# First layer's modulation on quarters of TensorE's columns, with a fixed order of the first products

## The chip, the cores and the metric

The kernel runs on one core of a Trainium2 chip. The metric is the device time of one execution in microseconds (us). Below, PE is TensorE, DVE VectorE, ACT ScalarE, POOL GpSimd, and SP the engine whose queue issues nearly all DMAs.

## The reference, cut to what matters

The reference is a network of two blocks of two layers each, on 256 context tokens and 256 latent tokens with 1024 channels, in float32. Only the very beginning matters here. Two conditioning vectors (one for the latents, one for the context) are turned into six modulation vectors of 1024 values by a product with a 1024 x 6144 matrix; the first two of these, shift and scale, go into the first norm, whose result is the input of the first projection:

```python
c_act = jax.nn.silu(c)
cc_act = jax.nn.silu(c_ctx)
for l in range(DEPTH):
    mod = (c_act @ w_mod[l] + b_mod[l])[:, None, :]
    modc = cc_act @ w_mod[l] + b_mod[l]
    sh1, sc1, g1, sh2, sc2, g2 = jnp.split(mod, 6, axis=-1)
    shc1, scc1, gc1, shc2, scc2, gc2 = jnp.split(modc, 6, axis=-1)
    px = (rmsnorm(x, norm1_g[l]) * (1.0 + sc1) + sh1) @ w_in[l] + b_in[l]
    pc = (rmsnorm(xc, norm1_g[l]) * (1.0 + scc1) + shc1) @ w_in[l] + b_in[l]
    ...
```

The gates of a linear recurrence (mLSTM), its keys, queries and values, a gated unit over groups and a convolution are columns of that projection.

## The kernel before, in words

Channels lie on partitions, tokens on the free axis: the input is eight tiles `xT` of 128 x 512 (columns 0 to 255 context, 256 to 511 latents). A projection splits its weights and its input into a high and a low part (`whi`, `wlo`, `aH`, `aL`; L391 loads a tile of weights, L392 and L397 split it) and does three products for each pair of pieces (`mm3`, L411 to L413). The program is written with a framework that orders each engine's instructions by a priority (the place in the program's text, moved by `high_priority(offset=...)`) and by when it believes them to be ready; the result is one fixed order for each engine, with semaphore waits. `issue_after(ins)` adds nothing but an order: what its block puts on the engine of `ins` is queued behind `ins`.

The stage in question is `start` (from L198), followed by `mixer1(0, ...)`:

- `__init__` loads small constants (L105 to L113, all on SP's queue); `start` loads two rows with the conditioning vectors (`crow`, L207) and the eight tiles `xT` (L210). `cvec_pe` (L138, L139) spreads the conditioning vectors over all partitions by products with a row of ones, and ACT applies the silu; the result `cv` is what the dot products on DVE need.
- The statistics of the first norm: squares on ACT (L212), their sum on DVE (L217), a sum over partitions on PE (`npc`, L323), a chain of small DVE operations (`rsq`, from L294), a product that spreads the factor by token (`npb`, L331), and eight products `xr` on DVE (L242).
- The modulation comes in pairs of tiles of 128 values, numbered q = 0 to 3, for scale (part 1) and shift (part 0). All scales and the pair 1 of the shifts are done by `mod_pe`: two weight blocks `mn` of 512 KB (L177), four products each (L180) with two columns stationary and 256 values streamed, so eight accumulating products into a 2 x 256 row `pR`, a copy by ACT (`mrow`, L182), two transposes on PE (`pM`, L184), and `mod_take` on DVE (L191, L196). The other six tiles of shifts are done by `mod_tile`: a block of 512 KB (L162) and one long DVE dot product for each of the two streams (L165).
- For each q ACT then applies scale and shift (`xn`, L255), and `split_plain` gives `aH` and `aL` (L378, L379). Eight buffers `mn` serve all these weight blocks. The first three weight tiles of the projection (`self.pre`) are loaded after pair 1.
- In `mixer1` the first three outputs (the gates, k0 and k1, called p3 below) are accumulated together by `accA`: eight input tiles x three outputs x three products, 72 products of 512 columns. Then `evac` takes the gates, a chain of small operations on DVE and ACT forms running sums and maxima (L727 to L765), and PE spreads them (`ptr`, L764, `pmi`, L759). The projection's further outputs follow in the order of `PLAN[0]`.
- The parts 2, 3 and 5 of the first layer's modulation (24 tiles, two dot products each on DVE, L165, blocks `mw`) are queued in `self.bg` and emitted by `work`. Part 4 is done by `mods`, with the same `mod_pe`, at a priority lowered by `LOW` = 300.

Of the kernel before, what the change touches and what calls it, by code (L numbers as in the profile page):

```python
# [18 lines left out]
D = 1024  # L19
KT = 8  # L20
# [10 lines left out]
# columns of the per-partition vectors of a layer of the first block  # L31
# [14 lines left out]
# constants  # L46
CS = {"ident": (0, 128), "mf": (128, 128), "mb": (256, 128)}
NCS = 384
# [14 lines left out]
SHPE = (1,)  # L63
# [24 lines left out]
class Net:  # L88
    def __init__(self, ctx, tc, i, o):
# [12 lines left out]
        self.late, self.long, self.pre, self.begun = [], None, [], []  # L102
        self.bg, self.credit, self.fence = [], 0.0, None
# [7 lines left out]
        nc.sync.dma_start(out=self.gn, in_=i["gn"])  # L111
        self.mb_t = g.tile([128, 4, 48], F32, name="modb")
        nc.sync.dma_start(out=self.mb_t, in_=i["modb"])  # L113
# [11 lines left out]
    # ---- modulation vectors: n on partitions, one dot product along the free axis each  # L125
# [5 lines left out]

    def cvec_pe(self, s, row):
        """The same for the first block, spread by the tensor engine."""
        nc = self.nc
        t = self.cv[s] = self.mp.tile([128, D], F32, tag="cv", name=f"cv0{s}")
        for h in range(2):
            p = self.mm_tile("pcv")
            nc.tensor.matmul(out=p, lhsT=self.ones[0:1, :], rhs=row[0:1, 512 * h:512 * h + 512], start=True, stop=True)  # L138
            nc.scalar.activation(out=t[:, 512 * h:512 * h + 512], in_=p, func=AF.Silu)  # L139
# [32 lines left out]
    def mod_pe(self, c, q, room, pr, pm):  # L172
        """Tiles 2 q and 2 q + 1 of the first layer's part c on the tensor engine, for both streams: rows, then turned."""
        nc = self.nc
        for h in range(2):
            w = room()
            nc.sync.dma_start(out=w, in_=self.i["modn"][PE_C.index(c), q, h])  # L177
            for n in range(4):
                k = 4 * h + n
                nc.tensor.matmul(out=pr, lhsT=self.cols[:, 2 * k:2 * k + 2], rhs=w[:, 256 * n:256 * n + 256], start=k == 0, stop=k == KT - 1)  # L180
        row = self.np_.tile([128, 256], F32, tag="xn", name="mrow")[0:2, :]
        nc.scalar.copy(out=row, in_=pr)  # L182
        for j in (0, 1):
            nc.tensor.transpose(out=pm[:, 2 * (2 * q + j):2 * (2 * q + j) + 2], in_=row[:, 128 * j:128 * j + 128], identity=self.ident[0:2, 0:2])  # L184
# [1450 lines left out]
```

## Time and profile before

| what | before |
|---|---|
| median of 3 runs (lowest, highest) | 2061.7 us (2060.18, 2063.29) |
| span of the profiled execution | 2055.1 us |
| median of the runs less that span | 6.6 us |
| PE busy, share of the span | 98% |
| DVE, ACT, POOL busy, share of the span | 75%, 45%, 4% |

The span reaches from the first to the last instruction of one profiled execution, and the page gives no other time for it; what a run's time has beyond it lies outside the instructions. A busy time is the union of an engine's instructions. PE's instructions overlap in it, since a product's record begins before the one ahead of it has ended: how fast PE works is read from the distance between starts, or from the length of a row of many.

### The profile page before, as it was taken

The numbers are of one execution on the slowest core, as the hardware profiler recorded it, in microseconds if no ns is written. First come the engines' busy times: TensorE is split into PE (matmuls) and PEld (weight loads), VectorE is DVE, ScalarE is ACT, GpSimd is POOL, SyncE is SP. The second block draws the span as 40 slices with busy tenths as digits, with TensorE's granted clock in tenths as the row PEclk, the third lists the DMA queues.
The fourth block names the chain that finished last, engine by engine and source line by source line (L and its number), as shares of the span: only waits on it lengthen the run. The fifth ranks groups of instructions, "written<-read, shape, count | busy, mean of one in ns | idle before, by whom it ended". The sixth has DMA issues, their size and how long they took to land.

```text
span 2055.1 us, 34137 instructions
## 1 busy us (share of the span) xinstructions
PE 2010.6 (98%) x13196; PEld 1784.5 (87%) x13196; DVE 1545.2 (75%) x3105; ACT 924.5 (45%) x1612; POOL 85.7 (4%) x103
## 2 busy tenths in 40 slices
PE   8999999999999899999999999999999999999999
PEld 3798779888888799999998789888888889999999
DVE  6997789987898768987877667777653487788554
ACT  4324544222322346744556675322222266666443
POOL 0000010000001000200100002000000200001000
PEclk9999999999999999999999999999999999999999
DMA  7532265678766332576651015446752231216554
GB/s 295 181 103 92 97 232 176 211 248 295 235 216 198 111 102 94 170 263 212 202 171 61 22 41 186 154 149 223 260 170 71 70 112 64 73 54 224 182 157 134
DMA packets 98182, 324.22 MB, mean 158 GB/s; under 512 B 11418, under 2 KB 14234, under 8 KB 98020
## 3 DMA queue, kind: packets, MB, share of 16 engines
q1 hardware_dynamic: 98020, 322.04, 47.7%
q8 instruction: 104, 1.70, 0.3%
q14 instruction: 58, 0.48, 0.1%
HBM read 320.95 MB, written 1.05 MB: 157 GB/s over the span
## 4 chain that ended last, share of the span: by engine, by line
PE 89%; DVE 6%; ACT 2%; DMA 1%; issue 1%; SPq 0%; POOL 0%; ACTq 0%; POOLq 0%; DVEq 0%
PE pg L411 6%; PE pd L411 6%; PE pd L413 6%; PE pd L412 6%; PE pu L413 6%; PE pg L412 6%; PE pu L412 6%; PE pg L413 6%; PE pu L411 6%; PE pin L411 5%; PE pin L413 5%; PE pin L412 5%; PE pov L1223 2%; PE ptq L1127 2%; DVE wlo L397 1%; PE po L411 1%
## 5 line engine op out<-in xcount | busy, mean ns | idle before, releaser
L392 ACT CAST whi<-wraw 128x1024 fp32r<-128x1024 f32 (+2 forms) x443 | 429.5, 973 | 797.0 <-PE pu L412 188.9
L397 DVE TENSOR_TENSOR wlo<-wraw,whi 128x1024 fp32r<-128x1024 f32 (+2 forms) x443 | 502.5, 1138 | 155.0 <-ACT whi L392 152.3
L165 DVE CUSTOM_DVE_ANT_0 junk<-mw,cv,modb 128x1024 bf16<-128x1024 f32 x272 | 349.6, 1285 | 51.3 <-DMA mw<-in_modw 45.2
L411 PE MATMUL pd<-hH,whi 128*128 128x256 f32 (+1 forms) x748 | 245.4, 328 | 0.0
L412 PE MATMUL pd<-hL,whi 128*128 128x256 f32 (+1 forms) x748 | 245.1, 328 | 0.0
L413 PE MATMUL pd<-hH,wlo 128*128 128x256 f32 (+1 forms) x748 | 244.8, 327 | 0.0
L411 PE MATMUL pg<-aH,whi 128*128 128x256 f32 (+1 forms) x704 | 233.8, 332 | 0.3 <-ACT aH L374 0.3
L413 PE MATMUL pu<-aH,wlo 128*128 128x256 f32 (+1 forms) x704 | 233.5, 332 | 0.3 <-DVE wlo L397 0.3
L412 PE MATMUL pg<-aL,whi 128*128 128x256 f32 (+1 forms) x704 | 233.6, 332 | 0.0
L412 PE MATMUL pu<-aL,whi 128*128 128x256 f32 (+1 forms) x704 | 233.2, 331 | 0.0
L411 PE MATMUL pu<-aH,whi 128*128 128x256 f32 (+1 forms) x704 | 233.2, 331 | 0.0
L413 PE MATMUL pg<-aH,wlo 128*128 128x256 f32 (+1 forms) x704 | 233.2, 331 | 0.0
L412 PEld LDWEIGHTS pd<-hL,whi 128*128 128x128 f32 x748 | 142.2, 190 | 12.2
L411 PEld LDWEIGHTS pd<-hH,whi 128*128 128x128 f32 x748 | 142.4, 190 | 12.0
L413 PEld LDWEIGHTS pd<-hH,wlo 128*128 128x128 f32 x748 | 142.2, 190 | 12.0
L411 PE MATMUL pin<-whi,aH 128*128 128x256 f32 x512 | 150.0, 293 | 1.4 <-ACT aH L374 1.1
L412 PE MATMUL pin<-wlo,aH 128*128 128x256 f32 x512 | 148.0, 289 | 0.0
L413 PE MATMUL pin<-whi,aL 128*128 128x256 f32 x512 | 147.2, 289 | 0.3 <-DVE aL L375 0.2
L411 PEld LDWEIGHTS pg<-aH,whi 128*128 128x128 f32 x704 | 133.7, 190 | 13.2 <-ACT aH L374 0.5
L413 PEld LDWEIGHTS pu<-aH,wlo 128*128 128x128 f32 x704 | 133.7, 190 | 13.1 <-DVE wlo L397 0.5
L413 PEld LDWEIGHTS pg<-aH,wlo 128*128 128x128 f32 x704 | 133.8, 190 | 12.6
L412 PEld LDWEIGHTS pg<-aL,whi 128*128 128x128 f32 x704 | 133.8, 190 | 12.5
(339 smaller groups left out, 4150.8 us busy)
## 6 DMA issues: line engine op xcount, KB each, us to landing
wraw<-in_wgu SPq DMA_DIRECT2D x176, 512.0 KB, 4.4
mw<-in_modw SPq DMA_DIRECT2D x168, 512.0 KB, 4.2
wraw<-in_win SPq DMA_DIRECT2D x92, 512.0 KB, 3.5
wraw<-in_wdn SPq DMA_DIRECT2D x64, 384.0 KB, 3.5
wraw<-in_wout SPq DMA_DIRECT2D x47, 512.0 KB, 3.5
wraw<-in_wdn SPq DMA_DIRECT2D x64, 320.0 KB, 3.4
mn<-in_modn SPq DMA_DIRECT2D x18, 512.0 KB, 5.6
mn<-in_modw SPq DMA_DIRECT2D x6, 512.0 KB, 7.3
```

The costliest lines, as they stand in the source:

```text
L165: r = nc.vector.tensor_tensor_reduce(out=junk, in0=w, in1=self.cv[s], scale=1.0, scalar=self.mb_t[:, 2 * b + l, j:j + 1], op0=ALU.mult, op ...
L392: nc.scalar.copy(out=hi[:, :n], in_=raw[:, :n])
L397: nc.vector.tensor_tensor(out=lo[:, :n], in0=raw[:, :n], in1=hi[:, :n], op=ALU.subtract)
L411: mm(out=out, lhsT=wh, rhs=xh, start=start, stop=False)
L412: mm(out=out, lhsT=wh, rhs=xl, start=False, stop=False)
L413: mm(out=out, lhsT=wl, rhs=xh, start=False, stop=stop)
L1127: nc.tensor.transpose(out=pt[:, h, :], in_=a.bitcast(F32).rearrange("p e d -> p (e d)"), identity=self.ident)
L1223: nc.tensor.matmul(out=po[64 * b:64 * b + 64, e // 2, :], lhsT=vN[:, kc, 64 * g:64 * g + 64], rhs=u["PT"][:, kc, :], start=kc == 0, stop=k ...
```

## The change

`mod_pe` no longer accumulates its eight products into one row of two partitions. It writes four products at a time to the four quarters (32 partitions each) of the output, with stationary operands padded with zeros to 32 columns (`columns`), and accumulates only over the two weight blocks; two products with a constant of two columns (`quart`), which has ones at the partitions 32 n + s, then add the four partial sums and turn the row at once, in place of the transposes. In `start` all eight tiles of the shifts are done in this way too, so `start` has no dot products on DVE, and the conditioning vectors spread over the partitions are not made there: two broadcast loads and two silus (`cvecs(0)`) make them, at the head of `self.bg`, with a priority lowered by 150. Each pair's products are queued on PE behind those of the pair before; 18 of p3's products (those of the input tiles 0 and 1) are queued between the pairs 2 and 3, and the other 54 behind pair 3. ACT's work for pair 2 is queued behind the last split of the three weight tiles. The constants' loads move from SP's queue to ACT's. The diff's core (comments, which it also removes, are left out):

```diff
-        self.cols = g.tile([128, 4 * KT], F32, name="cols")
+        self.cols = g.tile([128, KT, 2], F32, name="cols")
         nc.sync.dma_start(out=self.cols, in_=i["ccol"])
-        nc.scalar.activation(out=self.cols, in_=self.cols, func=AF.Silu)
...
-        nc.sync.dma_start(out=self.cst, in_=i["cst"])
+        nc.scalar.dma_start(out=self.cst, in_=i["cst"])
...
+    def columns(self, pool):
+        t = pool.tile([128, KT, 32], F32, name="cols32")
+        self.nc.gpsimd.memset(t, 0.0)
+        self.nc.vector.tensor_copy(out=t[:, :, 0:2], in_=self.cols)
+        return t
...
-    def mod_pe(self, c, q, room, pr, pm):
+    def mod_pe(self, cols, c, q, room, pr, pm):
         nc = self.nc
         for h in range(2):
             w = room()
             nc.sync.dma_start(out=w, in_=self.i["modn"][PE_C.index(c), q, h])
             for n in range(4):
-                k = 4 * h + n
-                nc.tensor.matmul(out=pr, lhsT=self.cols[:, 2 * k:2 * k + 2], rhs=w[:, 256 * n:256 * n + 256], start=k == 0, stop=k == KT - 1)
-        row = self.np_.tile([128, 256], F32, tag="xn", name="mrow")[0:2, :]
+                nc.tensor.matmul(out=pr[32 * n:32 * n + 32, :], lhsT=cols[:, 4 * h + n, :], rhs=w[:, 256 * n:256 * n + 256],
+                                 start=h == 0, stop=h == 1)
+        row = self.np_.tile([128, 256], F32, tag="xn", name="mrow")
         nc.scalar.copy(out=row, in_=pr)
         for j in (0, 1):
-            nc.tensor.transpose(out=pm[:, 2 * (2 * q + j):2 * (2 * q + j) + 2], in_=row[:, 128 * j:128 * j + 128], identity=self.ident[0:2, 0:2])
+            r = nc.tensor.matmul(out=pm[:, 2 * (2 * q + j):2 * (2 * q + j) + 2], lhsT=row[:, 128 * j:128 * j + 128], rhs=self.C("quart"),
+                                 start=True, stop=True)
+        return r.ins
...
-            for s, row in enumerate(rows):
-                self.cvec_pe(s, row)
...
-            def scale(q):
-                for c in (1, 0) if q in SHPE else (1,):
+            cols = self.columns(mf)
+            def part(q):
+                for c in (1, 0):
...
-            def shift(j):
-                if j // 2 not in SHPE:
-                    self.mod_tile(0, 0, j, (1, 0), room())
-            for j in range(2):
-                shift(j)
-            scale(0)
+            last = part(0)
             npb = self.rstd_rows([acc], T, 1.0 / D, pc, pb)
...
             for q in range(4):
-                with self.tc.issue_after(npb.ins):
-                    if q:
-                        scale(q)
-                for j in (2 * q, 2 * q + 1):
-                    if j >= 2:
-                        shift(j)
+                if q == 3:
+                    p3 = [self.mm_tile("pin") for _ in self.pre]
+                    with self.tc.issue_after(last):
+                        last = self.accA(p3, self.pre, (self.aH[:2], self.aL[:2]), ALL, True, False)
+                if q:
+                    with self.tc.issue_after(last):
+                        last = part(q)
                 if q == 1:
                     self.pre = [self.weights(self.i["win1"][0][j]) for j in range(3)]
-                for k in (2 * q, 2 * q + 1):
+                with ExitStack() as after:
+                    if q == 2:
+                        after.enter_context(self.tc.issue_after(self.whi))
+                    for k in (2 * q, 2 * q + 1):
...
+            self.first = (p3, last)
...
-                    p3 = [self.mm_tile("pin")[:, :cs[1] - cs[0]] for _ in w3]
-                    self.accA(p3, w3, (self.aH, self.aL), cs)
+                    if last:
+                        p3 = [self.mm_tile("pin")[:, :cs[1] - cs[0]] for _ in w3]
+                        self.accA(p3, w3, (self.aH, self.aL), cs)
+                    else:
+                        p3, ins = self.first
+                        with tc.issue_after(ins):
+                            self.accA(p3, [[a[:, 256:] for a in w] for w in w3], (self.aH[2:], self.aL[2:]), cs, False)
...
             def mods():
                 pm = self.mm_tile("pm")
+                cols32 = self.columns(tp)
                 for q in range(4):
-                    self.mod_pe(4, q, lambda: self.mp.tile([128, D], F32, tag="mw", bufs=2, name="mn"), pm[0:2, 0:256], pm[:, 256:272])
+                    self.mod_pe(cols32, 4, q, lambda: self.mp.tile([128, D], F32, tag="mw", bufs=2, name="mn"), pm[:, 0:256], pm[:, 256:272])
...
         self.start()
+        def vectors():
+            with self.tc.high_priority(offset=-150):
+                self.cvecs(0)
+        self.bg.append((0, vectors, None))
         self.mod_queue(0, 0, [j for j in range(16, 48) if j // 8 not in PE_C], (0, 1))
```

## Rows read from the trace of the kernel before

**Rows 1.** The profile's page: busy us by engine, share of the span, instructions.

```profile
PE 2010.6 (98%) x13196; PEld 1784.5 (87%) x13196; DVE 1545.2 (75%) x3105; ACT 924.5 (45%) x1612; POOL 85.7 (4%) x103
```

**Rows 2.** Stages (from:to, length): busy PE, PEld, DVE, ACT, POOL, clock, DMA, GB/s.

```profile
0.00:20.00 20.00, 12.14 (x24) 5.25 (x25) 10.17 (x17) 7.99 (x14) 0.91 (x7) 1.00 0.85 300
120.00:160.00 40.00, 40.00 (x268) 36.98 (x268) 40.00 (x89) 9.12 (x10) 0.00 (x0) 1.00 0.27 90
270.00:300.00 30.00, 26.05 (x199) 25.32 (x198) 28.27 (x48) 13.22 (x18) 5.54 (x6) 0.94 0.79 263
```

**Rows 3.** PE in order of time (start, length, instructions), 0 to 58 us.

```profile
4.35 7.16 PE L138 MATMUL pcv<-crow,ones 1*128 1x512 f32 x8 [4.35 <-DMA crow<-in_cvec]
14.77 1.86 PE L323 MATMUL npc<-ones,sqa 128*128 128x1 f32 x8 [3.25 <-DVE sqa L217]
16.89 5.87 PE L180 MATMUL pR<-mn,cols 128*2 128x256 f32 x16 [0.26 <-DMA mn<-in_modn]
24.48 3.62 PE L180 MATMUL pR<-mn,cols 128*2 128x256 f32 x16
46.18 0.50 PE L411 MATMUL pin<-aH,whi 128*128 128x512 f32 x1
...
57.63 0.39 PE L413 MATMUL pin<-aH,wlo 128*128 128x512 f32 x1
```

**Rows 4.** The same, the first part's weight loads (PEld), 17 to 18 us.

```profile
17.27 0.13 PEld L180 LDWEIGHTS pR<-mn,cols 128*2 128x2 f32 x1 [0.30 <-issue]
17.70 0.13 PEld L180 LDWEIGHTS pR<-mn,cols 128*2 128x2 f32 x1 [0.30 <-issue]
```

**Rows 5.** DMA, 0 to 75 us: rate in 40 slices of 1.875 us; issues by line.

```profile
GB/s 5 155 194 309 300 326 398 419 415 404 415 411 406 409 417 406 402 417 354 288 385 415 380 42 0 0 0 0 35 218 305 398 48 267 256 339 258 13 229 50
mn<-in_modn SPq DMA_DIRECT2D x10, 512.0 KB, 8.8
mn<-in_modw SPq DMA_DIRECT2D x6, 512.0 KB, 7.3
```

**Rows 6.** SP's queue in order of time: the first issue, and those of xT.

```profile
0.75 0.39 SPq L105 DMA_DIRECT2D cols<-in_ccol  x1
3.26 3.67 SPq L210 DMA_DIRECT2D xT<-in_xT  x8
```

**Rows 7.** PE late in the first mixer: products with 64 columns, then with 128.

```profile
218.24 1.09 PE L924 MATMUL psg<-sws,vs 128*64 128x128 f32 x16
219.26 1.09 PE L862 MATMUL pht<-cst,hs 128*128 128x128 f32 x8
```

**Rows 8.** In order of time, ACT and PE: three weight splits; a part's copy and turn.

```profile
28.73 2.93 ACT L392 CAST whi<-wraw 128x1024 fp32r<-128x1024 f32 x3
45.18 0.36 ACT L182 COPY mrow<-pR 2x256 f32<-2x256 f32 x1 [0.73 <-PE pR L180]
45.97 0.28 PE L184 MATMUL pM<-cst,mrow 2*128 2x2 f32 x2
```

**Rows 9.** Stages, dot products of L165 alone: DVE busy us (two records each).

```profile
0.00:52.50 52.50, 15.47 (x24) 1.00 0.77 288
52.50:58.00 5.50, 3.88 (x6) 1.00 0.55 184
```

**Rows 10.** The gates' chain in order of time: dot products in it, PE's wait.

```profile
65.62 1.27 DVE L165 CUSTOM_DVE_ANT_0 junk<-mw,cv,modb 128x1024 bf16<-128x1024 f32 x1
75.58 1.28 DVE L165 CUSTOM_DVE_ANT_0 junk<-mw,cv,modb 128x1024 bf16<-128x1024 f32 x1
77.68 0.28 PE L764 MATMUL ptr<-cst,RT 100*128 100x100 f32 x1 [3.31 <-issue]
```

**Rows 11.** Part 4 in the mixer, PE in order of time: a run, then single products.

```profile
222.33 2.75 PE L180 MATMUL pm<-mn,cols 128*2 128x256 f32 x12
251.98 0.59 PE L180 MATMUL pm<-mn,cols 128*2 128x256 f32 x2
252.82 0.59 PE L180 MATMUL pm<-mn,cols 128*2 128x256 f32 x2
```

More of the change, by code (lines that the diff above doesn't have):

```diff
@@ L45 @@
 NR2 = 776
-CS = {"ident": (0, 128), "mf": (128, 128), "mb": (256, 128)}
-NCS = 384
+CS = {"ident": (0, 128), "mf": (128, 128), "mb": (256, 128), "quart": (384, 2)}
+NCS = 386
 CG = {"sel": (0, 512), "reset": (512, 512)}
@@ L62 @@
 PE_C = [0, 1, 4]
-SHPE = (1,)
 WPRI = {"m1": 50, "ev": 400}
@@ L102, in __init__ @@
         self.late, self.long, self.pre, self.begun = [], None, [], []
+        self.whi = None
         self.bg, self.credit, self.fence = [], 0.0, None
-        self.cols = g.tile([128, 4 * KT], F32, name="cols")
+        self.cols = g.tile([128, KT, 2], F32, name="cols")
         nc.sync.dma_start(out=self.cols, in_=i["ccol"])
-        nc.scalar.activation(out=self.cols, in_=self.cols, func=AF.Silu)
         self.cst = g.tile([128, NCS], F32, name="cst")
-        nc.sync.dma_start(out=self.cst, in_=i["cst"])
+        nc.scalar.dma_start(out=self.cst, in_=i["cst"])
         self.ident = self.C("ident")
         self.gn = g.tile([128, 9, KT], F32, name="gn")
-        nc.sync.dma_start(out=self.gn, in_=i["gn"])
+        nc.scalar.dma_start(out=self.gn, in_=i["gn"])
         self.mb_t = g.tile([128, 4, 48], F32, name="modb")
-        nc.sync.dma_start(out=self.mb_t, in_=i["modb"])
+        nc.scalar.dma_start(out=self.mb_t, in_=i["modb"])
+        nc.scalar.activation(out=self.cols, in_=self.cols, func=AF.Silu)
         self.cv = [None, None]
@@ L130, in cvec @@
         nc.scalar.activation(out=t, in_=t, func=AF.Silu)
[L132 to L139, printed above, removed]
     def cvecs(self, b):
@@ L204, in start @@
             pc, pb, pR, pM = [pp.tile([128, T], F32, name=n) for n in ("npc", "npb", "pR", "pM")]
-            rows = [mf.tile([1, D], F32, name=f"crow{s}") for s in range(2)]
-            for s, row in enumerate(rows):
-                nc.sync.dma_start(out=row, in_=self.i["cvec"][s:s + 1, :])
+            pR = [pR, self.ps.tile([128, T], F32, tag="aux", bufs=1, name="pR1")]
             acc = None
@@ L218, in start @@
                     acc = a2
-            for s, row in enumerate(rows):
-                self.cvec_pe(s, row)
             A, m = self.modA[0, 0, 1], self.mod[0, 0]
@@ L243, in start @@
             for q in range(4):
-                with self.tc.issue_after(npb.ins):
-                    if q:
-                        scale(q)
-                for j in (2 * q, 2 * q + 1):
-                    if j >= 2:
-                        shift(j)
+                if q == 3:
[5 more added lines that the diff above has]
+                        last = part(q)
                 if q == 1:
                     self.pre = [self.weights(self.i["win1"][0][j]) for j in range(3)]
-                for k in (2 * q, 2 * q + 1):
-                    t = mf.tile([128, T], F32, tag="t", bufs=2, name="xn")
-                    for s, (c0, c1) in ((1, CTX), (0, LAT)):
-                        nc.scalar.activation(out=t[:, c0:c1], in_=xr[k][:, c0:c1], func=AF.Identity,
-                                             bias=m[:, s, k:k + 1], scale=A[:, s, k:k + 1])
-                    self.split_plain(t, self.aH[k], self.aL[k])
+                with ExitStack() as after:
+                    if q == 2:
+                        after.enter_context(self.tc.issue_after(self.whi))
+                    for k in (2 * q, 2 * q + 1):
+                        t = mf.tile([128, T], F32, tag="t", bufs=2, name="xn")
+                        for s, (c0, c1) in ((1, CTX), (0, LAT)):
+                            nc.scalar.activation(out=t[:, c0:c1], in_=xr[k][:, c0:c1], func=AF.Identity,
+                                                 bias=m[:, s, k:k + 1], scale=A[:, s, k:k + 1])
+                        self.split_plain(t, self.aH[k], self.aL[k])
+            self.first = (p3, last)
     def mod_queue(self, b, l, tiles, streams):
@@ L391, in weights @@
         nc.sync.dma_start(out=raw[:, :n], in_=src)
-        nc.scalar.copy(out=hi[:, :n], in_=raw[:, :n])
+        self.whi = nc.scalar.copy(out=hi[:, :n], in_=raw[:, :n]).ins
         up = WPRI.get(self.phase)
@@ L412, in mm3 @@
         mm(out=out, lhsT=wh, rhs=xl, start=False, stop=False)
-        mm(out=out, lhsT=wl, rhs=xh, start=False, stop=stop)
+        return mm(out=out, lhsT=wl, rhs=xh, start=False, stop=stop).ins
     def accA(self, outs, ws, xs, cols, first=True, last=True):
@@ L422, in accA @@
             for out, w in zip(outs, ws):
-                self.mm3(out, w[0][:, q], w[1][:, q], H[k][:, c0:c1], L[k][:, c0:c1], first and k == 0, last and k == n - 1)
+                r = self.mm3(out, w[0][:, q], w[1][:, q], H[k][:, c0:c1], L[k][:, c0:c1], first and k == 0, last and k == n - 1)
+        return r
     def accB(self, out, ws, t):
@@ L1517, in lay @@
     cc = np.stack([f("c")[0], f("c_ctx")], axis=1)
-    out["ccol"] = np.concatenate([cc.reshape(KT, 128, 2).transpose(1, 0, 2).reshape(128, 2 * KT)] * 2, axis=1)
+    out["ccol"] = cc.reshape(KT, 128, 2).transpose(1, 0, 2)
     mb = np.stack([f("b_mod"), f("mod_b_2")]).reshape(4, 48, 128)
@@ L1530, in lay @@
     cst[:, 256:384] = np.where(p >= q, 0.0, NEG)
+    for n in range(4):
+        for st in range(2):
+            cst[32 * n + st, 384 + st] = 1.0
     out["cst"] = cst
```

3 lines of the change are left out of this document (2 added, 1 removed).

## The prediction, made before the changed kernel was run

> **What bounds the kernel now.** The page comes first: PE is busy 98% of the span [rows 1], so what counts is PE's own work and the few places where PE has nothing to do or works slowly. The stages come second. The first 20 us hold little PE work, the middle of the first mixer has PE and DVE both full, and at 270 to 300 us PE idles for 4 us [rows 2]. The change touches nothing after the first mixer, so third comes the order of time on PE from 0 to 82 us. PE spreads the conditioning vectors, sums the squares, does the first part of the modulation in 5.87 us and four more in 3.62 us each, and ends p3 at 58.0 [rows 3]. From 24.5 us to there it hardly stops: its own queue bounds the start, not the loads, whose rate falls to nothing after 43 us [rows 5]. After p3 comes a wait of 3.31 us for the gates' chain on DVE, which holds dot products that nothing there needs [rows 10]. From 82 to 270 us PE has no gap.
>
> **What the start becomes.** Per part (eight products, 16 records), PE needs 15 steps of 0.216 us and a tail, 3.62 us [rows 3]. The nearest row for quarters is for halves: 16 records with 64 columns each, to alternating halves, take 1.09 us, exactly what 8 records with 128 columns take [rows 7]. So two halves run side by side. For quarters I take four at a time, so a part costs 4 steps, 0.87 us; the other end is no overlap at all, 3.46 us. The parts in the start go from five (17.3 us) to eight (7.0 us). The 12 dot products of the start, 15.47 us of DVE [rows 9], and the spread, 7.16 us of PE, go; the latter lay under the wait for xT, so it is worth nothing.
>
> PE then no longer bounds the start, and **what is late next is the last weight block**. The volume does not change: 10 + 6 blocks before [rows 5], 16 after. With xT (8 x 262 KB by its shape), three weight tiles of 524 KB and 0.34 MB of constants, 12.4 MB must land ahead of p3's last 54 products. The rates of rows 5 add up to 11.6 MB after 18 slices (33.75 us), and 0.8 MB more at 0.41 MB/us ends at 35.6 us. SP issues one load ahead of xT in place of six, and xT was first issued 2.5 us after the first load [rows 6]; I take 1.3 us of this, between 0 and 2.5. The last block lands at 34.3 us. The eight buffers should not break the stream: the loads of pair 3 wait for the products of pair 1, whose blocks land by about 20 us on the same curve, and 3.6 MB stand in the queue behind them, 8.8 us of loading.
>
> Behind the last block come four products in two steps (0.43 us), ACT's copy (0.36), the turn (0.28) [rows 8] and some 0.4 us of hand-over: 1.5 us. Then 54 products: 51 of them start within 11.45 us of each other from first to last [rows 3], 0.229 us each, so 12.4 us. p3 ends at 34.3 + 1.5 + 12.4 = 48.2 in place of 58.0: **9.8 us gained**.
>
> The 18 products queued ahead of pair 3 (4.1 us) must fit before 34.3. Their weights land at about 24 us (8.2 MB on the curve), ACT's splits take 2.93 us [rows 8] and DVE's last subtraction about 1.2, so they can run from 28 to 32. The splits of input tiles 6 and 7 follow the last block by 5 us, and PE reaches tile 6 only 8 us after it: hidden; without this cover they would cost 3 us. The wider copy on ACT has the same 256 columns for each partition, so I take 0.36 for it as well. Padding on POOL, the constants on ACT's queue and the quarter-sum constant lie under xT's loading; without that cover they cost about 1 us. For ACT's pair 2, queued behind the weight splits, 2.93 us are not late while pair 2's blocks land at about 29.
>
> **What the first mixer becomes.** The conditioning vectors now arrive by two broadcast loads of 0.5 MB and two silus. They are issued when the start's loads are through, and nothing on PE waits for them, but the dot products do: three ran ahead of p3's end [rows 9], three more in the gates' chain. If they come late enough, the gates' chain loses the three that stand in it (two are in rows 10), 3.9 us of DVE, and PE's wait of 3.31 us. If they are ready by then, they fill the same gaps. Between 0 and 3.3 us gained I take 1.0, since DVE is idle earlier, which speaks for their being early, while the lowered priority speaks for late.
>
> Part 4 has 64 records at 0.216 us, 13.8 us of PE; four at a time they would be 3.5, a gain of 10.4. But the rows show one long run of 12 records, two of six, and 20 single products (two records), each with one projection product between [rows 11]. A single quarter has nothing to run beside. The three runs hold 12 products, 5.2 us, which become four steps of 0.43, 1.7 us. I take **3.5 us**, between 0 and 10.4; the reason is that nothing in the change ties part 4's products together.
>
> The single ones pass 0.84 us from one to the next [rows 11], 0.43 their own and about 0.12 the projection product's, so 0.3 us goes into two changes of form. The Trainium skill (TensorEngine Tiling (Array Packing), Key Properties) says that a change of the tiling mode drains the engine. The halves of rows 7 show no loss within their run or to the next. By the rule, a drain of the size of these changes at each of some 16 entries and exits in the start would add up to 2 us to PE, under the wait for blocks, and the sum would stay as it is but for the last one, 0.1 us.
>
> **The sum.** 9.8 + 1.0 + 3.5 = 14.3 us. The profiled execution spans 2055.1 us, so the changed kernel's would span 2040.8. The median of the three runs is 2061.7, 6.6 us above that span; with the same 6.6 us I predict **2047 us**. About 0.2% (4.1 us) is what a measurement of this kernel can tell from no change.
>
> **Rivals.**
> All comes true: the chain loses its dot products (3.3), part 4 runs four and four (10.4), with xT a little earlier (10.5): 24 us, 2037.5. Against it stand the single products of rows 11.
>
> TensorE stays slow in the start. The windows row gives a granted clock of 1.00 for 0 to 20 us [rows 2], but the first part's steps are 0.43 us [rows 4], twice the later 0.216: the lower of the two levels. PE rose to the upper one in the midst of the first part (5.87 us long), after working without a gap since 14.77. With quarters PE works for 0.87 us, 1.7 at the lower level, while two blocks take 2.6 us to land. If it is still at the lower level when the 18 products begin at 28 us, they take 8.2 us, and pair 3 follows at about 36 and needs some 4 us with its two hand-overs; the 54 start at 40 and end at 52.5. The gain is 5.5, the total 10, 2052. The Trainium skill (TensorE: Matmul & The Clock Gate, Part 1) says that the lower level is the default and that idling brings it back; by that rule this case is the likelier one, and the trace agrees as far as the first part goes.
>
> DVE takes over. It is full at 120 to 160 us [rows 2], and the change moves up to six dot products, 8 us, from before 77 us into that stretch while PE arrives 10 us earlier. If the convolution on DVE is then late for PE, the lead is spent: 2060. Against it: no PE wait at 120 to 270 us is put down to DVE.
>
> Quarters do not overlap (slower). Then eight parts cost 27.7 us of PE or more, and PE bounds the start again: pair 0 takes about 10 us from 14, at first at the low level, the pairs 1 and 2 about 8 each with hand-overs, then 4.1 for the 18, 8 for pair 3 and 12.4: p3 ends near 65, 7 us later than now, 2069. It decides as soon as a part costs over 2.5 us or so. The halves of rows 7 speak against it.
>
> **Numbers.** The forecast has 0.54, the slow clock 0.20, all true 0.12, DVE 0.08, no overlap 0.06. The forecast's own bounds (block 1.3 us earlier or later, chain 0 to 3.3, part 4 from 0 to 7) give 2040 to 2053; with the slow clock and most of the first rival the range is 2037 to 2056. Faster: forecast, clock and all true, 0.86, of which a point goes to the bounds; same: DVE, 0.08; slower: 0.07.
>
> **What would show it.** Each part's 16 records of L180's successor within 1.1 us, in four starts; the last weight block landing at 33 to 36 us; p3's last product at about 48 us; no dot product before 40 us; part 4 in the mixer partly in groups. Wrong would be steps that are serial, the 18 products at 0.43 us each, p3 ending after 53, or a new PE wait on DVE between 120 and 200 us.

## The result, and the profile after

The changed kernel takes 2073.0 us (median of 4 runs, 2069.8 to 2075.2), the kernel before in the same comparison 2060.9: ratio 1.0058, 95% interval 1.0043 to 1.0074. It is **slower, by some 12 us**, where 14 us of gain were forecast. Its profiled execution spans 2070.4 us. (Wherever the time and the span of one run are both known, they lie 1.7 to 2.2 us apart. So of the 6.6 us between median and span in the section on the time before, only some 2 lie outside the instructions; the rest says that the profiled execution of before is a quick one.) On the page PE's busy time falls by 7 us and DVE's by 14 [rows 1]:

```profile
PE 2003.6 (97%) x13266; PEld 1794.0 (87%) x13266; DVE 1531.3 (74%) x3086; ACT 925.2 (45%) x1613; POOL 81.2 (4%) x105
```

So less work takes longer. Where the time is lost shows when the same product of PE starts in both traces (counted among the products with the same operands):

| PE's product | before | after | lag |
|---|---|---|---|
| last of p3 | 57.63 | 62.71 | +5.1 |
| 54th of pin from aH and wlo, behind the gates' chain | 86.28 | 94.90 | +8.6 |
| first of po (the mixer's output projection) from aH and wlo | 227.53 | 236.12 | +8.6 |
| 24th of the next stage (pg from aH and whi) | 327.84 | 340.58 | +12.7 |
| 232nd of the same, now in the second layer | 889.98 | 905.67 | +15.7 |
| last of the kernel from hH and whi (pd) | 2050.56 | 2066.21 | +15.7 |

Three places, then: the start, the end of the first mixer (in which part 4 lies), and 3 us in the second layer. The two profiled executions lie 15 us apart; the medians, 12, since before's is the quick one.

**The start.** PE in order of time (start, length, instructions; in brackets the wait ahead and what ended it):

```profile
20.32 1.93 PE L178 MATMUL pR<-mn,cols 128*32 128x256 f32 x16
...
29.56 1.07 PE L178 MATMUL pR<-mn,cols 128*32 128x256 f32 x16
36.28 1.01 PE L183 MATMUL pM<-cst,mrow 128*128 128x2 f32 x4 [5.64 <-ACT mrow L181]
37.22 1.93 PE L178 MATMUL pR<-mn,cols 128*32 128x256 f32 x16
40.52 0.77 PE L410 MATMUL pin<-aH,whi 128*128 128x512 f32 x1
41.09 0.63 PE L411 MATMUL pin<-aL,whi 128*128 128x512 f32 x1
...
50.10 0.61 PE L183 MATMUL pM<-cst,mrow 128*128 128x2 f32 x4 [0.46 <-ACT mrow L181]
50.57 0.48 PE L410 MATMUL pin<-aH,whi 128*128 128x512 f32 x1
...
62.71 0.39 PE L412 MATMUL pin<-aH,wlo 128*128 128x512 f32 x1
...
82.51 0.40 PE L769 MATMUL ptr<-cst,RT 100*128 100x100 f32 x1 [3.05 <-DVE RT L753]
```

The 16 records of a part lie within 1.07 us at PE's upper clock level (1.93 at the lower), against 3.62 in [rows 3]: quarters do run side by side. But the products of pair 2's first half, the scale, are done by 30.6, and their turn starts only at 36.28. It waits for one copy on ACT:

```profile
30.37 1.03 ACT L391 CAST whi<-wraw 128x1024 fp32r<-128x1024 f32 x1
31.31 0.60 ACT L253 ACTIVATE xn<-xr,mod,modA 128x256 f32<-128x256 f32 x1
31.81 1.03 ACT L391 CAST whi<-wraw 128x1024 fp32r<-128x1024 f32 x1
32.75 0.61 ACT L377 CAST aH<-xn 128x512 fp32r<-128x512 f32 x1
33.27 0.60 ACT L253 ACTIVATE xn<-xr,mod,modA 128x256 f32<-128x256 f32 x1
33.77 1.03 ACT L391 CAST whi<-wraw 128x1024 fp32r<-128x1024 f32 x1
...
35.34 0.62 ACT L377 CAST aH<-xn 128x512 fp32r<-128x512 f32 x1
35.86 0.37 ACT L181 COPY mrow<-pR 128x256 f32<-128x256 f32 x1
```

The copy stands behind the three weight splits and pair 1's scaling and splits. These begin only at 29.87, as pair 1's last turn on PE ends at 29.64: the parts before it stand one behind the other's turn, and until about 26 us they run at the lower level (1.93 us). Behind the wait PE is slow again: the first eight of the 18 products start 0.43 us apart, the others 0.23. Part by part of the stage (columns as in [rows 2]):

```profile
30.00:34.00 4.00, 0.63 (x12) 0.13 (x4) 2.35 (x2) 4.00 (x7) 0.00 (x0) 0.98 0.98 367
34.00:44.00 10.00, 7.23 (x32) 5.18 (x33) 3.73 (x8) 5.64 (x11) 0.00 (x0) 0.50 0.78 261
80.00:92.00 12.00, 9.49 (x34) 7.70 (x35) 7.45 (x19) 2.42 (x3) 0.31 (x1) 0.57 0.35 108
```

PE is idle nearly throughout 30 to 34 us, and then the granted clock is 0.50, the lower level, for ten. It falls again with the 3.05 us wait for the gates' chain. The Trainium skill (TensorE: Matmul & The Clock Gate, Part 1) says that idling brings the lower level back; the trace agrees at these two places. A wait of 3.0 to 3.3 us at the gates does not always bring it: before had none behind its 3.31 us [rows 10], and the experiments have both.

**The end of the mixer.** Stages of before, then of after:

```profile
190.00:266.00 76.00, 76.00 (x475) 55.18 (x475) 55.51 (x167) 38.10 (x84) 2.52 (x2) 1.00 0.27 90
266.00:300.00 34.00, 30.05 (x227) 28.61 (x226) 32.27 (x54) 14.41 (x22) 6.61 (x7) 0.95 0.77 256
280.00:290.00 10.00, 8.95 (x60) 8.69 (x60) 9.09 (x16) 2.99 (x5) 0.46 (x1) 0.83 0.72 226
```

```profile
190.00:266.00 76.00, 75.52 (x525) 61.31 (x524) 57.27 (x159) 40.78 (x90) 2.61 (x3) 1.00 0.31 99
266.00:300.00 34.00, 23.04 (x161) 20.81 (x160) 30.07 (x68) 10.77 (x19) 3.91 (x3) 0.80 0.67 218
280.00:290.00 10.00, 1.43 (x9) 1.27 (x10) 10.00 (x18) 1.36 (x2) 0.26 (x1) 0.65 0.74 232
```

Up to 266 us PE gets through 50 more instructions than before in the same 76 us. Then it falls from 30 us of work to 23, and between 280 and 290 it all but stops while DVE is busy for 10.00 of 10. The waits of PE from 260 to 330 us (total, times, longest) name it:

```profile
PE pht L867 <- DVE hs L860: 7.2, 1, 7.2
```

What DVE does there (in order of time):

```profile
268.20 0.16 DVE L293 TENSOR_SCALAR nw_a<-pss 128x4 f32<-128x4 f32 x1
...
270.12 1.28 DVE L156 CUSTOM_DVE_ANT_0 junk<-mw,cv,modb 128x1024 bf16<-128x1024 f32 x1 [0.49 <-DMA mw<-in_modw]
...
286.62 0.15 DVE L310 SCALAR_TENSOR_TENSOR nw_y<-nw_u,nw_y 128x4 f32<-128x4 f32 x1
286.70 1.22 DVE L396 TENSOR_TENSOR wlo<-wraw,whi 128x1024 fp32r<-128x1024 f32 x1
287.83 1.28 DVE L156 CUSTOM_DVE_ANT_0 junk<-mw,cv,modb 128x1024 bf16<-128x1024 f32 x1
289.04 0.69 DVE L860 TENSOR_TENSOR hs<-hs,nw_y 128x512 f32<-128x512 f32 x1
```

The chain of the last head norm, from its first operation (L293) to its product (L860), takes 20.8 us. Nine of the ten last dot products of part 3 (the second norm's shifts) and four weight splits stand between its operations. Before, the same chain ran from 254.27 to 260.2 and the ten dot products came after it; PE still had part 4 to do.

### The profile page after: what moved, and what is told of

The parts are those of the page before. It is cut to its first block, busy times and chain, and to the rows that moved or that the text cites. A ratio compares the mean times of both kernels' runs of the same rounds, so it can differ in the third digit from the quotient of the medians.

```text
span 2070.4 us, 34271 instructions
## 1 busy us (share of the span) xinstructions
PE 2003.6 (97%) x13266; PEld 1794.0 (87%) x13266; DVE 1531.3 (74%) x3086; ACT 925.2 (45%) x1613; POOL 81.2 (4%) x105
## 4 chain that ended last, share of the span: by engine, by line
PE 86%; DVE 8%; ACT 2%; issue 2%; DMA 1%; SPq 0%; POOL 0%; POOLq 0%; ACTq 0%; DVEq 0%
PE pg L410 6%; PE pu L412 6%; PE pg L411 6%; PE pg L412 6%; PE pu L410 6%; PE pu L411 6%; PE pd L410 6%; PE pd L411 6%; PE pd L412 6%; PE pin L410 4%; PE pin L412 4%; PE pin L411 4%; DVE wlo L396 2%; PE pov L1229 2%; PE ptq L1133 2%
## 5 line engine op out<-in xcount | busy, mean ns | idle before, releaser
L411 PEld LDWEIGHTS pd<-hL,whi 128*128 128x128 f32 x748 | 142.3, 190 | 12.2
L411 PEld LDWEIGHTS pg<-aL,whi 128*128 128x128 f32 x704 | 134.4, 191 | 12.4
```

What stands on the lines that cost most here:

```text
L411: mm(out=out, lhsT=wh, rhs=xl, start=False, stop=False)
```

## The experiments

Every ratio is against the kernel before on the same chip; a time "by ratio" is (ratio - 1) x 2060 us, so after stands at +11.9. A ratio's interval is 2 to 3 us to either side, so the difference of two ratios is known to some 4 us. The edits are to the changed kernel unless said otherwise.

### Which part loses the time

x1: part 4 as before (two columns, one row, transposes), the new start alone. x2: the kernel before with part 4 on quarters alone.

```diff
-  self.mod_pe(cols32, 4, q, ..., pm[:, 0:256], pm[:, 256:272])
+  self.mod_pe2(4, q, ..., pm[0:2, 0:256], pm[:, 256:272])     # x1: L171 to L184 of before
```

> Before stood at 2060.9 us and after at 2073.0, 12.0 more. Here the start is as in after, and part 4 in the mixer is computed as before (two columns, one running sum, two transposes). My theory reads three terms off the two traces: the start costs 5.1 us at the first products' end and 8.6 behind the gates, part 4 on quarters gives back some 12, and the chain of the last head norm, which the vector engine then runs with dot products between its small operations, costs some 16. By it this kernel is 2060.9 + 8.6 = 2069.5 us (2066 to 2073), with the lag of 5.1 us at the first 72 products' end, the old products of part 4, and no wait of 7 us for the head norm. The rival, that the start's loss is absorbed by waits further on and all of the 12 us comes from the mixer, gives 2061 us.

> The kernel before, with nothing but part 4 in the mixer on quarters of the columns. By my theory it gains some 12 us up to 266 us, and loses some 16 to the head norm's chain, in which the dot products then stand: 2060.9 - 12 + 16 = 2065 us (2060 to 2069). The rival, that the dot products came into the chain because the changed start made them late, gives a gain that stays: 2049 us (2047 to 2053).

Measured: x1 1.0032 [1.0018, 1.0046], +6.6 us; x2 1.0016 [1.0002, 1.0030], +3.3. **Each half loses by itself**; together they lose 11.9. Part 4, whose term ran from 0 to 10.4 us of gain, costs time even with the old start. In x2's trace the last head norm's chain, now from 265.68 to 284.93, has eight of the ten dot products and three weight splits in it, as after's has; x1 has none there.

### What the mixer's end loses

x3 queues the ten dot products behind the norm's product; x5 leaves them out (five tiles of the second norm's shift then hold the bias only); x12 and x15 leave them out of before, and of x2.

```diff
+  ("hnorm", 3), ("hnorm", 2), ("behind",), ("work",), ("work",), ("gated", 2), ...   # x3; behind: self.fence = that product
-  ("work",), ("work",), ("step", 3, 0, ...), ...
```
```diff
+  if (b, l) == (0, 0) and 27 <= j < 32:                         # x5, x12, x15, in mod_tile
+      for s in streams: nc.vector.tensor_copy(out=m[:, s, j:j + 1], in_=self.mb_t[:, 0, j:j + 1])
+      return
```

> After, with the ten dot products that stand in the last head norm's chain queued behind that chain; nothing else is moved. By my theory the tensor engine's wait of 7.2 us for the head norm goes, and with it the stretch at the low clock: the lag at the first feed-forward products falls from 12.7 us to some 0 (-3 to +4), and the time from 2073.0 to 2060 us (2057 to 2065). The rival, that the vector engine is full there and the same work is only late elsewhere (the gated products, the splits or the next norm wait for the dot products instead), leaves 2070 to 2073 us.

> After, in which the last five of the mixer's tiles of dot products (tiles 27 to 31 of the first layer's modulation, ten dot products of 1.28 us, 12.8 us of the vector engine, and their 2.6 MB of loads) are left out: those entries take the bias alone. Putting them behind the head norm's chain took the wait of 7.2 us away but gave only 3.7 us, and a wait of 5.8 us for a weight split came up. The theory now: the vector engine is full in 266 to 300 us, since part 4's 12 us on the tensor engine had hidden its work, so only fewer of its instructions help. By it this kernel gains 10 us on after: 2063 us (2058 to 2066), with the lag of 12.7 us at the first feed-forward products down to 0 to 3. The rival, that after the head norm the loads or the clock decide and not the vector engine, leaves it where the move behind the chain did: 2069 us.

> The kernel before, with the same ten dot products left out (the same five tiles take the bias alone). Theory: before had part 4's 12 us on the tensor engine beside that work, so the dot products are mostly covered there: 0 to 6 us less than before, 2057 us (2053 to 2060). The rival, that these ten dot products cost before as much as after, whatever part 4 does, gives 2040 us (2037 to 2045).

> The kernel before, with part 4 on quarters and the same ten dot products left out (five tiles take the bias alone). With the start of before, it shows what part 4's quarters give where the vector engine is not full: by the theory some 6 to 10 us on the kernel before without the ten dot products (2053.9 us), 2046 us (2043 to 2050); the difference to after without them (2052.5 us) is then the start's cost. The rival, that part 4 is hidden anyway, gives 2053 us.

x3, expected at 2060 us, took 2069.3, 1.0046 [1.0034, 1.0058]: the 7.2 us wait is gone, but DVE is as full as before, and a new wait takes its place (the stage, then PE's product):

```profile
280.00:290.00 10.00, 3.39 (x23) 2.66 (x21) 10.00 (x18) 2.36 (x4) 0.73 (x1) 0.79 0.55 177
```

```profile
290.49 0.58 PE L412 MATMUL po<-aH,wlo 128*128 128x256 f32 x1 [5.83 <-DVE wlo L396]
```

So it looks like the amount and not the order: the weight splits now wait where the norm did. Without the ten: x5 0.9972 [0.9960, 0.9985], x12 0.9964 [0.9952, 0.9977], x15 0.9929 [0.9914, 0.9944]. In x5, where no dot product is left there, PE has 9.40 us of work in the stage that was empty:

```profile
280.00:290.00 10.00, 9.40 (x76) 9.18 (x77) 9.14 (x21) 6.20 (x8) 1.89 (x2) 1.00 0.95 316
```

The ten dot products, 12.8 us of DVE, cost the kernel before 7.4 us, after 17.7, and x2 17.9 (1.0016 less 0.9929). And without them **part 4 on quarters is worth 7.2 us** (x12 less x15).

### What the start loses

x4: ACT's weight splits behind pair 2's copies. x14: five products of a 128 x 128 block of ones with xT, used by nothing, in PE's long wait. x7: each part's products ahead of the turn of the part before, the weights' high halves on DVE, the 18 products as 9 and 9, the dot products behind the gates' chain.

```diff
+  if q == 1: self.pre = [self.load(...) for j in range(3)]               # x4
+  if q == 2:
+      with self.tc.issue_after(self.mcopy): self.pre = [self.halve(*x) for x in self.pre]
```
```diff
+  for n in range(5): f = nc.tensor.matmul(out=self.fill, lhsT=self.ones, rhs=self.xT[n], ...).ins   # x14
+  e.enter_context(self.tc.issue_after(f))                                 # then the turn
```
```diff
+  ORDER = "p1 t0 p2 t1 p3 t2 w p4 t3 p5 t4 p6 k0 t5 k1 p7 t6 t7"          # x7: p products, t turn and xn, w weights, k nine products
```

> After, with the three weight splits on the scalar engine behind part 2's two copies; the loads stay where they are. By my theory the tensor engine's 5.64 us wait for part 2's copy goes and the clock stays up in 34 to 44 us, so that the first 72 products end 5 to 9 us earlier (54 to 58 us instead of 63.1) and the time is 2073.0 - 7 = 2066 us (2063 to 2069). The rival, that the weights' splits or part 3's blocks are then the late ones, moves the wait to the 18 products or to part 3 and leaves 2070 to 2073 us.

> After, with five further products of the ones with the squares' inputs (128 x 512 in float32, some 0.93 us each at the high clock, into a bank that is no longer read) on the tensor engine in the 5.64 us for which it waits for part 2's copy. They change no result. It asks for the clock alone: if the low clock of 34 to 44 us comes from the engine's idling, the granted clock stays at 1.00 in 30 to 46 us, the first 72 products end some 3 us earlier (60 instead of 63.1) and the time is 2070 us (2068 to 2072). If the clock falls there for another reason, nothing changes: 2073 us, and up to 2076 if the fillers delay the turn.

> After, with the start put in another order: the products of half n + 1 stand ahead of the turn of half n, the hi halves of the first three weight blocks are made by the vector engine, nine of the first products stand behind half 6 of 8 and nine behind the next turn, and the dot products stand behind the gates' chain. By my theory of the start (the scalar engine's copy behind the splits, and every half's products behind the turn of the one before) the first 72 products end at 54 to 57 us instead of 63.1, the clock stays up behind the gates more often, and the time is 2073 - 9 = 2064 us (2060 to 2068). The rival, that the start is bound by the blocks' loads (16 blocks of 512 KB and the rest, up to some 35 us) and then by the 72 products at the low clock, leaves the end at 60 to 63 us and 2070 to 2073 us.

x4: 1.0043 [1.0031, 1.0055], 3 us better than after, which is not clear of the intervals. The wait shrinks to 1.94 us, but the splits are later now, and the 18 products start at 39.37, barely earlier; PE's parts take 1.93 us up to there. x14: 1.0036 [1.0023, 1.0049], 4.5 better, just clear, with 5.35 us of work that nothing needs:

```profile
31.11 1.93 PE L178 MATMUL pR<-mn,cols 128*32 128x256 f32 x16
32.97 5.35 PE L186 MATMUL npc<-xT,ones 128*128 128x512 f32 x10
38.15 0.50 PE L194 MATMUL pM<-cst,mrow 128*128 128x2 f32 x4
38.58 1.07 PE L178 MATMUL pR<-mn,cols 128*32 128x256 f32 x16
...
40.61 0.48 PE L422 MATMUL pin<-aH,whi 128*128 128x512 f32 x1
```

The part behind it takes 1.07 us where after's took 1.93. The 18 products still begin at 40.61, as in after, and p3's last comes at 61.10, 1.6 earlier. But x14's PE was slow up to the filler (1.93 at 31.11, where after had 1.07), so its copy came at 37.40, 1.5 later than after's. x17, with after's start, was slow up to there as well, its copy came at 37.52 and p3's last at 64.05: against this one the filler gains 3.0 us. The start's order weighs more than the clock behind that wait: x7, nearly all of whose parts up to 35.83 take 1.9 us too, still brings p3's last to 57.55, 6.5 ahead of x17 and 0.1 ahead of before. It changes several things at once, so ACT's queue and the order of parts and turns are not told apart. Its time is 1.0033 [1.0022, 1.0044]: the gates' chain is not ready for p3, and the wait for the last norm, 7.11 us, is still there.

```profile
73.74 0.40 PE L787 MATMUL ptr<-cst,RT 100*128 100x100 f32 x1 [3.98 <-DVE RT L771]
75.13 2.74 PE L782 MATMUL pmi<-mi,sel 4*128 4x4 f32 x16
```

The 16 small products behind that wait take 2.74 us; behind x17's 3.03 us wait, without a fall of the clock, 1.52.

### Ways to take the dot products off DVE's last stage

x6: part 3 on PE too, with part 4's code. x8: x6 and x7. x9: the conditioning vectors spread by PE as before, ten dot products of part 2 (its tiles 16 to 20) in the start. x10: x9 in x7's start. x11: x10, and the gates' small products at a lower priority. x13: the kernel before with parts 3 and 4 on quarters. In all six the last two `work` calls go.

```diff
-PE_C = [0, 1, 4]                                    # x6, x8, x13
+PE_C = [0, 1, 3, 4]
```
```diff
+  for j in range(16, 21): self.mod_tile(0, 0, j, (0, 1), room())        # x9; x10, x11: among the parts
```

> After, with the second norm's shifts (eight tiles, sixteen dot products) computed on the tensor engine with part 4, in the same quarters, and the last two calls for dot products in the mixer dropped; the dot products that were queued behind come then in the feed-forward phase. By the theory of the full vector engine it loses the ten dot products in 266 to 300 us (-10) and pays four more pairs of halves on the tensor engine (some 4 x 1.4 = 5.6 us): 2068 us (2063 to 2071). By the rival (loads or clock decide, and the tensor engine's additional work comes on top) 2073 to 2078 us.

> The two last kernels in one: the pipelined start, and the second norm's shifts on the tensor engine. If the two terms are independent, the sum is 2073 - 9 - 5 = 2059 us (2053 to 2064), about the time before (2060.9). If what the start gives is only slack for the vector engine further on, the sum is less than its parts: 2064 us or more.

> Leaving the ten dot products out gave after 20 us back, more than their own 12.8 us. So the vector engine's work behind the head norms is the bound there, and the change had emptied the vector engine in 40 to 60 us (3.4 us busy of 20) and left it full in 268 to 300 us. This kernel is after with the condition vectors spread by the tensor engine as in the kernel before, five tiles of dot products done in the start, behind part 3, and the mixer's last two calls for dot products dropped. No work is left out. Theory: most of the 20 us comes without leaving anything out: 2056 us (2052 to 2061), lag at the first feed-forward products some -3 to +3 us instead of 12.7. The rival, that ten dot products in 45 to 62 us delay the first splits and the gates' chain by as much, gives 2064 to 2072 us.

> The dot products in the start as in the last kernel, and the pipelined start (products of half n + 1 ahead of the turn of half n, hi halves on the vector engine). If the start's gain (first 72 products' end 5 us earlier) is kept once the vector engine is not full behind the head norms, 2056 - 5 = 2051 us (2046 to 2056), below before's 2060. If the gates' chain or the mixer takes it back, 2056 us.

> The last kernel, with the gates' eight selector products and four transposes at a lower priority, so that they come some 30 products later on the tensor engine, which waits 3 to 4 us for them in every kernel so far and then often runs at the low clock. Theory: 3 to 5 us less than the last kernel: 2046 us (2042 to 2052). Rival (the wait moves to the first step's exponentials): no difference to the last kernel.

> The kernel before with its own start; parts 4 and 3 of the modulation in the mixer on quarters, and the mixer's last two calls for dot products dropped. If the start's cost (some 5 to 8 us) and the full vector engine (some 17 us) are all that took part 4's gain away, this one is faster than before: 2060 - 10 (part 4) + 5.6 (part 3's products) - 4 (ten dot products, covered only in part before) = 2052 us (2048 to 2057). If the wait comes up again in the next stage, 2058 to 2064 us.

| | ratio | p3's last | 54th of pin | 24th of pg |
|---|---|---|---|---|
| x6 | 1.0028 [1.0017, 1.0038] | 63.62 | 92.01 | 328.31 |
| x8 | 1.0020 [1.0006, 1.0034] | 58.43 | 91.57 | 330.51 |
| x9 | 1.0030 [1.0017, 1.0043] | 66.35 | 104.64 | 332.75 |
| x10 | 1.0030 [1.0020, 1.0040] | 67.08 | 96.98 | 330.33 |
| x11 | 1.0025 [1.0017, 1.0034] | 66.86 | 91.60 | 331.00 |
| x13 | 0.9987 [0.9973, 1.0001] | 57.63 | 90.03 | 327.37 |

The last two columns are the products of the first table; in x11 the gates' products come behind the 54th. x6 gains only 6 us on after: part 3 then loads PE instead. In x9 DVE is busy for 19.70 of 20 us:

```profile
60.00:80.00 20.00, 12.05 (x44) 9.48 (x43) 19.70 (x29) 6.37 (x7) 1.82 (x12) 0.74 0.50 174
```

PE waits 8.0 us there, for DVE's evacuation of the gates: the trouble of the mixer's end has moved to its beginning. In x10 and x11 p3 does not come earlier either, since the spread now stands ahead of the parts on PE. Four times (x8 to x11: 2065 to 2067 us, expected at 2046 to 2059) gains that were expected to add up did not; x13, at 2057.5, came 5 us short.

x16 to x18 put the two `work` calls of the ten dot products to where PE is full and DVE is not, 190 to 266 us (DVE 55.51 of 76, above); x16 with x2's part 4 and the old start, x17 in the changed kernel, x18 in the kernel before, as the control.

```diff
-  ("hnorm", 1), ("work",), ("conv_norm",)] ... ("work",), ("work",), ("step", 3, 0, ...)
+  ("hnorm", 1), ("work",), ("low", 100, "work"), ("low", 100, "work"), ("conv_norm",)] ... ("step", 3, 0, ...)
```

> The kernel before with its own start, part 4 on quarters, and the mixer's last two calls for dot products moved ahead of the convolution's norm at a lower priority, so that the ten dot products come in 190 to 266 us, where the tensor engine is full and the vector engine is busy some 7.5 of every 10 us. Nothing is left out. With the ten dot products left out it took 2046.3 us. Theory: most of that is kept: 2050 us (2046 to 2055), faster than before. The rival, that the dot products delay the mixer's own vector work by as much as they cost later, gives 2059 to 2064 us.

> After, with the same two calls moved ahead of the convolution's norm at a lower priority, nothing else. With the ten dot products left out it took 2052.5 us; so 2057 us (2053 to 2062), some 16 us less than after, the start's loss still in it. The rival gives 2068 to 2073 us.

> The control: the kernel before with the two calls moved alike, part 4 as it was. With the ten dot products left out it took 2053.9 us. Theory: 2056 us (2053 to 2061); what lies between this and the run with part 4 on quarters is part 4's own worth, some 7 us.

Measured: **x16 2046.7 us, 0.9933 [0.9917, 0.9948]**; x17 1.0001 [0.9987, 1.0015]; x18 0.9968 [0.9954, 0.9982]. In their traces the ten run from 176 to 203 us (x16), 191 to 215 (x17) and 181 to 208 (x18), and none between 266 and 300. The end of the mixer in x16, and in x17:

```profile
266.00:300.00 34.00, 31.55 (x254) 30.51 (x253) 31.14 (x60) 21.26 (x36) 11.10 (x8) 1.00 0.64 222
```

```profile
266.00:300.00 34.00, 32.48 (x266) 29.78 (x266) 28.82 (x61) 18.78 (x31) 7.20 (x6) 1.00 0.73 244
```

Both hold PE at over 31 us of 34, where after had 23.04. x16 beats both kernels, by 13.8 and 25.7 us. The move alone is worth 6.6 us before (x18), 11.7 after (x17) and 17.1 with part 4 on quarters (x2 to x16); part 4 on quarters beside it 7.2 (x18 to x16), as without the dot products. The new start costs 14.0 us between x16 and x17.

## Why the prediction was wrong

**The last weight block (right).** The last block lands at 35.4, for a forecast of 34.3 (33 to 36). In x4, where the next weight loads come later and don't hide it, the rate falls to nothing at 34 to 35 us (slices of 1 us from 20 us):

```profile
GB/s 406 430 414 418 430 406 438 406 418 430 406 410 404 281 41 0 0 0 0 0 0 61 287 246 197 324 365 328 377 406 41 0 0 16 0 18 216 183 261 270
```

**The quarters (right).** 1.07 us a part at the upper level, a little over the forecast 0.87. The drain at a change of the tiling mode, which the Trainium skill (TensorEngine Tiling (Array Packing), Key Properties) states, is not to be seen as a price: eight records among full-width products take 0.64 us.

**The step that failed first: "For ACT's pair 2, queued behind the weight splits, 2.93 us are not late while pair 2's blocks land at about 29."** They were late. The fixed order puts the copy, which PE needs at 30.6, at 35.86; with it goes the claim that the 18 products "can run from 28 to 32". They ran from 40.52 to 46.5. Against the forecast's p3 end at 48.2 this is 12.2 us (46.5 less 34.3); pair 3 behind them took 4.1 us (46.49 to 50.57) and not 1.5, 2.6 more; the 54 products took 12.5 for 12.4. Sum 14.9: 63.1 us, as measured. I had counted ACT's splits (2.93), but of pair 1's work, which alternates with them in the queue, nothing: four scalings and two splits more. And none of it begins before 29.87, though pair 1's last block had landed at 21.6 and the last weight tile at 25.3 (put at about 20 and 24). PE waits for no block in the start: it was late with pair 1 by itself, each part's products behind the turn of the one before and at the lower level. The prediction had no term for that order. In x7, which changes the order, p3's last comes 6.5 us ahead of x17's, with PE slow in both.

**The slow clock (rival, right in kind, and likelier than its 0.20).** It gave 52.5 for p3's end, but let the 18 products begin at 28. In after PE works at the lower level until about 26 us and again behind the wait. In x1, x5, x6 and x17, which share its start, it does so without a break until the 18 products, and p3's last comes at 63.62 to 65.92; after's 62.71 is, by luck, the earliest of the five. Behind the wait this costs 3.0 us of p3's end (x14 against x17). Ahead of it, it costs after some 3, an estimate from its rows: two parts of 1.93 for 1.07, the spread of the norm's factor 2.07 for 1.13, two turns of 0.85 and 1.01 for 0.61. So of the 14.9 us some 6 are the clock's and the rest the order's.

**The gates' chain.** One us of gain was taken; the wait shrank from 3.31 to 3.05, for four dot products stand in the chain as before (from 68 to 80 us; before from 63 to 76). The low clock behind the wait cost this execution 3.5 us (the lag goes from 5.1 to 8.6), but that is not the change's doing: in x5 and x17, with the same start and the same wait, there is no fall, and in x13 and x18, with the start of before and its wait of 3.3 us, there is one (the 16 small products take 2.74 and 2.75 us; before 1.52).

**Part 4, the second step that failed: 3.5 us were credited and nothing looked at what part 4's time on PE had covered.** Where it is not taken back, the gain is even larger: 7.2 us. But [rows 2] showed DVE at 28.27 of 30 us between 270 and 300, with ten dot products in it. Part 4 had kept PE busy up to 267.8 us (its last turn), and DVE had the last norm's chain behind it by then. With part 4 on quarters PE comes to the end sooner, and the chain falls among the dot products, with the new start (after) and with the old (x2, where PE's longest wait of the stage is 4.4 us, for the next norm's sum); x1, with the old part 4, has no such wait. So the same edit gains 7.2 us (x18 to x16) where the dot products are out of the way, and loses 3.3 (x2) where they are not.

**DVE takes over (rival).** The right engine, at 0.08, but placed at 120 to 160 us; there after has no such wait, and it came at 268 to 300.

The sum by ratio: +11.9 = the new start alone (x1) 6.6 + part 4 alone (x2) 3.3 + 2.0 that neither has by itself, which is within the intervals. So the start, forecast at -10.8, is the larger error, and part 4, forecast at -3.5, the smaller.

**What stays open.** The start's price is 6.6 us in one pair (x1), 8.9 in a second (x5 less x15), 14.0 in a third (x17 less x16), each known to some 3 to 4 us; p3's last lies at 64.1 to 65.9 in x1, x5 and x17, and which wait the clock falls at differs from one execution to the next, so the profiles, one each, don't settle it. The 3 us lost in the second layer follow a wait of PE for a norm's sum (2.6 us, before 0.9) with a granted clock of 0.83 behind it; x5 and x17 lose 3.0 and 2.7 there, x1 and x16 under 0.5. What makes that sum late is not shown. That DVE's amount of work, not PE's order, is the bound in 268 to 300 rests on x3, x5, x16 and x17; no run kept the norm's chain and the weight splits both clear of the dot products with all of them left in this stage.

## What to carry to other kernels

When a step on the busiest engine becomes shorter, list what the other engines did under it, and price that work anew at the place where it then stands; the step's own gain comes only when the cover is no longer needed (here: by doing ten dot products some 80 us earlier). Where an order is fixed by hand, follow each queue, not the sum of its work: one 0.37 us copy behind nine operations held PE for 5.64 us. And an idle PE can pay twice, for the wait and for a slow stretch behind it: a start in which PE has little to do is better priced at the lower level.

## What the runs showed of the hardware

Work that nothing needs made the kernel faster: 5.35 us of products in a wait gained 4.5 us by ratio (x14), and 3.0 us of p3's end against x17. A wait of 3.0 to 3.3 us for the gates' chain was followed by slow products in some executions (after, x13, x18) and not in others (before, x5, x17). The granted clock of a stretch does not always tell the pace: in x17 it reads 1.00 from 34 to 44 us, while a turn and a product of p3 there take as long as in after at 0.50:

```profile
34.00:44.00 10.00, 5.57 (x28) 3.86 (x29) 4.48 (x8) 5.67 (x11) 0.00 (x0) 1.00 0.81 253
```

```profile
41.31 1.01 PE L183 MATMUL pM<-cst,mrow 128*128 128x2 f32 x4 [0.49 <-ACT mrow L181]
42.75 0.63 PE L411 MATMUL pin<-aL,whi 128*128 128x512 f32 x1
```

So the length of a known product is the surer sign, as [rows 2, 4] had it for the first 20 us of before. And a single quarter costs as much as four: two records 0.62 us, eight 0.64.
